# Last step of the block inverse split over both 64-partition halves, and the sample tokens' z with both parts of the rows in one left side

## The chip, the cores and the metric

The kernel runs on one core of one Trainium2 chip. The time is device time in microseconds (us) of one execution; a run is repeated and the median is given. The engines are named as in the profile: PE is TensorE's matmuls, PEld its weight loads (the left side of a matmul), DVE is VectorE, ACT is ScalarE, POOL is GpSimd, SP is SyncE, which here issues the DMAs.

## The reference

One inference step of one decoder layer, on a prompt of 2048 tokens and on 8 sample sequences of 4 tokens each (32 rows, which go along with the last pass over the prompt). An input projection of 1024 columns feeds two head groups: 16 state-space heads (SSD) and 8 gated delta-rule heads (GDN), each with a gate z that is a column block of the same projection.

```
h    = rmsnorm(x) * (1 + scale) + shift
proj = h @ w_in                       # z_s, xbc, dt, z_g, qkv, a, b
# GDN, in chunks of rows, per head:
M    = strict_lower((k*beta) @ k.T * decay);   A = I + M
u, w = solve(A, [v*beta, k*beta*exp(gcum)])    # unit lower triangular
v_new = u - w @ S;  o = q_dec @ S + attn @ v_new;  S = S*d + k_dec.T @ v_new
# SSD: y = chunked state-space scan, then y * silu(z_s), norm
o    = rmsnorm(o) * silu(z_g)
out  = x + gate * (concat(y, o) @ w_out);      y = rmsnorm(out)
```

The kernel uses chunks of 128 rows and forms the inverse of A for each chunk and head, by blocks: the four 32 x 32 diagonal blocks first, then pairs of them, then the 64 x 64 block off the diagonal. This last block is a product of three 64 x 64 matrices, made in two steps of one matrix product each.

## The kernel before

The prompt goes through in four passes of 512 tokens. All work of the passes is cut into small functions, each put at a due time with `at(tau, f)`; one unit of tau is a quantum, about one half of a projection tile, and a pass is 106 of them. The functions are run in order of tau. TensorE's instructions stay in just that order (`manual_schedule`); the other engines' order is made by the framework's scheduler from its own model of the times. SP issues nearly all DMAs, in one queue.

The projections are made with fp32r matmuls on parts: each fp32 value is a high part and a low part (`hhi`, `hlo` for the normed rows, two halves of a tile for the weights), and a product is high x high, high x low and low x high, added up in PSUM. `z_pair` makes two z tiles of 128 columns each in four quanta; in the last pass (`p == SP`) each quantum also makes the z of the 32 sample rows, into a PSUM buffer `d["s"]` that stays over the four quanta. `zmm` is the product of one slice k: three matmuls, with the rows as the left side (128 prompt rows, or 32 sample rows) and 256 weight columns moving. There are 8 z pairs, so 32 quanta in the last pass. At the end of a pair the z tiles go through ACT (tanh) and DVE (multiply-add); the sample's goes to `zsd` in DRAM.

`gdn_pair` carries two heads (b = 0, 1) through a pass: 4 chunks each, so 8 matrices in `U` (column index c = 4 b + chunk). After the diagonal blocks come the functions `b2_0` to `b2_4`: b2_0 transposes blocks, b2_1 and b2_2 make the 32 x 32 blocks off the diagonal in each 64 x 64 half, b2_3 and b2_4 the 64 x 64 block. b2_3 multiplies into partitions 64 to 127 of a PSUM buffer, ACT copies that to `p2x`; b2_4 multiplies into partitions 0 to 63 of another, DVE copies that into `U`. The functions b2_1 to b2_4 stand 1.45 quanta apart. After them come the `hop`s, three a chunk, which carry the state S through the chunks and read U in the second. There are 4 pairs in each of 4 passes, 16 in all.

PSUM has eight buffers: three of tag `ip` (projections), three of tag `bk` (b2, transposes, SSD chunks, the sample's z, and more, in turn), one `ch` and one `o` (hops). `ssd_group` has the SSD chunks; its function `second` (L1035) makes 8 heads' products of 64 columns, each in two matmuls of 64 left columns, one to partitions 0 to 63 and one to 64 to 127. `want` loads and splits the weights, four halves ahead (`NH = 4`). After the passes comes the output projection (L1185), with the sample tokens' own scans woven in.

Of the kernel before, what the change touches and what calls it, by code (L numbers as in the profile page):

```python
# [7 lines left out]
F32 = mybir.dt.float32  # L8
F32R = mybir.dt.float32r
AF = mybir.ActivationFunctionType  # L10
ALU = mybir.AluOpType
X = mybir.AxisListType.X

P = 128
DM = 1024
SEQ = 2048
KD = 8
T = 512
NPC = SEQ // T
NC = T // P  # L20
NS = 32
# [8 lines left out]
def _bc(ap, shape):  # L30
    while len(ap.shape) < len(shape):
        ap = ap.unsqueeze(len(ap.shape))
    return ap.to_broadcast(shape)
# [3 lines left out]
def hymba_step_kernel(  # L37
# [6 lines left out]
    v, s, g, pe = nc.vector, nc.scalar, nc.gpsimd, nc.tensor  # L44
    cnt = [0]

    def nm(t):
        cnt[0] += 1
        return f"{t}_{cnt[0]}"

    def mk(pool, shape, tag, dt=F32):
        return pool.tile(shape, dt, tag=tag, name=nm(tag))
# [13 lines left out]
    def psum(tag):  # L66
        return pools[tag].tile([P, 512], F32, tag=tag, name=nm("p" + tag))
# [20 lines left out]
    ct = const.tile([P, KD, 9], F32, name="ct")  # L88
# [28 lines left out]
    hw = ph1.enter_context(tc.tile_pool(name="hw", bufs=1))  # L117
    wp = ph1.enter_context(tc.tile_pool(name="wp", bufs=NH))
    xr = ph1.enter_context(tc.tile_pool(name="xr", bufs=3))
    keep = ph1.enter_context(tc.tile_pool(name="keep", bufs=1))  # L120
# [4 lines left out]
    trp = ph1.enter_context(tc.tile_pool(name="trp", bufs=4))  # L125
# [5 lines left out]
    def at(tau, f):  # L131
        events.append((tau, len(events), f))
# [16 lines left out]
            yield  # L149


    th9 = keep.tile([P, KD, 9], F32, name="th9")
    sc = keep.tile([P, KD, 9], F32, name="sc")
    s.activation(th9[:], ct[:], AF.Tanh, scale=0.5)
    v.tensor_scalar(sc[:], ct[:], 0.5, None, ALU.mult)
    v.scalar_tensor_tensor(sc[:], th9[:], 1.0, sc[:], ALU.add, ALU.mult)
    ADA = ("kT", "vs", "qd", "kd", "A", "U")
    ada_n = [0]

# [42 lines left out]
        return part  # L202


    hhi = hw.tile([P, KD, T + NS], F32R, name="hhi")
    hlo = hw.tile([P, KD, T + NS], F32R, name="hlo")
    wg2 = keep.tile([P, KD, 64], F32R, name="wg2")
    id2 = keep.tile([64, 32], F32, name="id2")
# [10 lines left out]
    dt2 = keep.tile([P, 8, 64], F32, name="dt2")  # L219
    p1x = keep.tile([P, 8, 64], F32, name="p1x")  # L220
    p2x = keep.tile([P, 8, 64], F32, name="p2x")
# [14 lines left out]
    def split(hi, lo, src):  # L236
        s.copy(hi, src)
        v.tensor_tensor(lo, src, hi, ALU.subtract)  # L238

    def rstd(ssq, n, scale):  # L240
        w = ssq.shape[1]
        m = mk(b2, [P, NC], "m1")[0:n, 0:w]
        v.tensor_scalar(m, ssq, scale, EPS, ALU.mult, ALU.add)
        r = mk(b2, [P, NC], "r1")[0:n, 0:w]
        rsq(r, m)
        return r
# [7 lines left out]
    def row_stats(src, n, ss, pool, tag):  # L254

        sh = mk(b2, [P, 2], "ssq2")
        xs = []
        for i in range(2):
            xt = mk(pool, [P, T], tag)
            nc.sync.dma_start(xt[0:n], src[:, i * 512:(i + 1) * 512])  # L260
            jk = mk(b1, [P, 512], "xsq", mybir.dt.bfloat16)
            s.activation(jk[0:n], xt[0:n], AF.Square, accum_out=sh[0:n, i:i + 1])
            xs.append(xt)
        v.tensor_tensor(ss, sh[0:n, 0:1], sh[0:n, 1:2], ALU.add)
        return xs
# [51 lines left out]
    def h_sample():  # L317
        ss = mk(b2, [P, 1], "ssq")[0:NS]
        xs = row_stats(x_s, NS, ss, xr, "xin")
        r = rstd(ss, NS, 1.0 / DM)  # L320
        pt = psum("bk")
        for i in range(2):
            v.tensor_scalar(xs[i][0:NS], xs[i][0:NS], r, None, ALU.mult)
            for k in range(4 * i, 4 * i + 4):
                pe.transpose(pt[:, k * NS:(k + 1) * NS], xs[i][0:NS, (k - 4 * i) * P:(k - 4 * i + 1) * P],
                             ident[0:NS, 0:NS])
        hv = mk(trp, [P, T], "tr")[:, 0:KD * NS]
        h4 = hv.rearrange("p (k b t) -> p k b t", k=KD, b=NB)
        v.tensor_tensor(h4, pt[:, 0:KD * NS].rearrange("p (k b t) -> p k b t", k=KD, b=NB),
                        _bc(s1[:, :, 1:9], [P, KD, NB, 4]), ALU.mult)  # L330
        v.tensor_tensor(h4, h4, _bc(mod[:, 0:8, 1:9], [P, KD, NB, 4]), ALU.add)
        split(hhi[:, :, T:T + NS], hlo[:, :, T:T + NS], hv.rearrange("p (k t) -> p k t", k=KD))

    state = {}

# [123 lines left out]
    n = 0  # L459
# [57 lines left out]
    def fill(tau, parts):  # L517
        d = {}
        fills.append((tau, parts, d))
        return d  # L520
# [63 lines left out]
    def z_pair(tau, n, p, mcol, done):  # L584

        d = fill(tau, [(n, j, True) for j in range(4)])

        def quantum(j):
            want(d["i0"] + j)
            ws = [w.rearrange("p (t k) c -> p t k c", t=2) for w in wt[d["i0"] + j]]  # L590
            for bk in range(2):
                if j == 0:
                    d[bk] = psum("ip")
                for k in range(2 * j, 2 * j + 2):
                    for i in range(2):
                        c = bk * 2 + i
                        cols = slice(c * P, (c + 1) * P)
                        zmm(d[bk][:, i * 256:(i + 1) * 256], k, cols, ws, i == 0)
            if p == SP:
                if j == 0:  # L600
                    d["s"] = psum("bk")
                for k in range(2 * j, 2 * j + 2):
                    zmm(d["s"][0:NS, 0:256], k, slice(T, T + NS), ws, True)
            if j == 3:
                zt = mk(b4, [P, NC, 256], "z")
                for bk in range(2):
                    zf = zt[:, bk * 2:bk * 2 + 2, :].rearrange("p a b -> p (a b)")
                    s.activation(zf, d[bk][:], AF.Tanh, scale=0.5)
                    v.scalar_tensor_tensor(zf, zf, 1.0, d[bk][:], ALU.add, ALU.mult)
                if p == SP:  # L610
                    zs_ = mk(trp, [P, T], "tr")[0:NS, 0:256]
                    s.activation(zs_, d["s"][0:NS, 0:256], AF.Tanh, scale=0.5)
                    v.scalar_tensor_tensor(zs_, zs_, 1.0, d["s"][0:NS, 0:256], ALU.add, ALU.mult)
                    nc.sync.dma_start(zsd[:, mcol:mcol + 256], zs_)
                done(zt)

        def zmm(out, k, cols, ws, first):
            for e, (a, b) in enumerate(((hhi, 0), (hhi, 1), (hlo, 0))):
                pe.matmul(out.rearrange("p (t c) -> p t c", t=2), a[:, k, cols], ws[b][:, :, k % 2, :],  # L619
                          start=(first and k == 0 and e == 0), stop=(k == KD - 1 and e == 2), skip_group_check=True)  # L620

        for j in range(4):
            at(tau + j, lambda j=j: quantum(j))


    def gdn_pair(p, pr, so, zq, e, dch):
# [225 lines left out]
        def b2_3():  # L852
            U = st["U"]
            pw = psum("bk")
            for c in range(8):
                pe.matmul(pw[64:128, c * 64:(c + 1) * 64], U[:, c, 64:128], dt2[:, c, :], start=True, stop=True)
            s.copy(p2x[64:128], pw[64:128, :].rearrange("p (c n) -> p c n", c=8))

        def b2_4():
            U = st["U"]  # L860
            pz = psum("bk")
            for c in range(8):
                pe.matmul(pz[0:64, c * 64:(c + 1) * 64], p2x[:, c, :], U[:, c, 64:128], start=True, stop=True)
            v.tensor_copy(U[0:64, :, 64:128], pz[0:64, :].rearrange("p (c n) -> p c n", c=8))

        at(so + 31.7 + e, b2_0)
        for i, f in enumerate((b2_1, b2_2, b2_3, b2_4)):
            at(so + 33 + e + 1.45 * i, f)
# [192 lines left out]
    for p in range(NPC):  # L1061
# [30 lines left out]
        if p + 1 < NPC:  # L1092
            for tt in range(NC):
                at(base + 60.4 + 4 * tt, lambda p=p, tt=tt: stat_tile(p + 1, tt, xr, "xin"))
            sr = stat_row(p + 1)
            for i in range(2):
                at(base + (93.6, 96.4)[i], lambda sr=sr: next(sr))
            if p + 1 == SP:
                at(base + 94.4, h_sample)
# [598 lines left out]
```

## Time and profile before

| | |
|---|---|
| median of 3 runs | 2328.43 us (2324.95 to 2330.56) |
| the profiled execution | 2327.78 us, span 2326.1 us |
| mean granted TensorE clock | 0.979 |
| TensorE matmuls | 15405, busy 2200.8 us (95% of the span) |
| weight loads | busy 1864.9 us (80%) |
| VectorE, ScalarE, GpSimd | 1481.9 (64%), 953.1 (41%), 826.7 us (36%) |
| DMA | 387.94 MB, mean 167 GB/s |

A busy TensorE is not one at its peak: a matmul's duration contains its way through the array, and the next begins before it ends, so what a group of matmuls takes from the program is read from the distance of their starts. In a group line of the profile stand line, engine, operation, tile written and tiles read, shapes (partitions x columns of the left side, then of the moving side), count, busy time, mean duration of one, and the idle time of the engine ahead of them with what ended it. An fp32 matmul of the program is two instructions in the profile, an fp32r one is one.

### The profile page before, as it was taken

How to read it: one execution, taken by the hardware profiler on the slowest of the kernel's cores; microseconds unless marked ns; L12 is line 12 of the kernel's file. 1: busy time of each engine (PE TensorE's matmuls, PEld its weight loads, DVE VectorE, ACT ScalarE, POOL GpSimd, SP SyncE). 2: the span in 40 equal slices, each digit the busy share in tenths (PEclk: the TensorE clock that was granted, in tenths of full speed). 3: DMA queues.
4: the chain of work that ended last, by engine and by line, in shares of the span. 5: the costliest groups of instructions: out<-in, count | busy, mean ns of one | idle time of the engine just before them, and what ended most of it. 6: DMA issues, size and time to landing. Idle time of an engine off the chain costs nothing. (4 is left out here: it accounts for less than half of the span.)

```text
span 2326.1 us, 41856 instructions
## 1 busy us (share of the span) xinstructions
PE 2200.8 (95%) x15405; PEld 1864.9 (80%) x15405; DVE 1481.9 (64%) x3574; ACT 953.1 (41%) x2680; POOL 826.7 (36%) x1052
## 2 busy tenths in 40 slices
PE   6999999989999999999999989999999799998998
PEld 3688878868897887889788889998899377786786
DVE  2466868786767768675666776668676564454323
ACT  2534556454536445442533453435433432231111
POOL 3255665554437243411522241215211554322000
PEclk8999999999999999999999999999999999999999
DMA  6354655555766675465645544555445563643321
GB/s 239 113 167 152 191 166 180 181 181 174 225 214 209 213 225 183 143 193 165 191 153 179 178 135 132 180 154 157 150 147 160 165 211 125 191 155 128 129 86 52
DMA packets 241112, 387.94 MB, mean 167 GB/s; under 512 B 75880, under 2 KB 132968, under 8 KB 240908
## 3 DMA queue, kind: packets, MB, share of 16 engines
q1 hardware_dynamic: 240908, 385.28, 52.2%
q8 instruction: 121, 1.98, 0.3%
q14 instruction: 83, 0.68, 0.1%
HBM read 289.89 MB, written 95.30 MB: 166 GB/s over the span
## 5 line engine op out<-in xcount | busy, mean ns | idle before, releaser
L531 PE MATMUL pip<-hhi,w 128*128 128x512 f32 (+1 forms) x2880 | 823.7, 362 | 6.7 <-DVE kT L549 4.9
L531 PEld LDWEIGHTS pip<-hhi,w 128*128 128x128 f32 x2880 | 515.0, 190 | 85.0 <-issue 6.9
L531 PE MATMUL pip<-hlo,w 128*128 128x512 f32 (+1 forms) x1440 | 509.8, 354 | 0.0
L619 PE MATMUL pip<-w,hhi 128*128 128x256 f32 x2048 | 382.6, 287 | 0.3 <-DVE cv L549 0.3
L496 POOL TENSOR_TENSOR w<-xin,w 128x512 fp32r<-128x512 f32 x156 | 202.6, 1301 | 378.3 <-ACT w L495 344.8
L619 PEld LDWEIGHTS pip<-w,hhi 128*128 128x128 f32 x2048 | 316.5, 190 | 2.4 <-DVE cv L549 0.5
L531 PEld LDWEIGHTS pip<-hlo,w 128*128 128x128 f32 x1440 | 274.5, 191 | 36.9 <-issue 4.5
L619 PE MATMUL pip<-w,hlo 128*128 128x256 f32 x1024 | 289.4, 283 | 0.0
L1185 PE MATMUL pip<-wohi,mh 128*128 128x512 f32 x480 | 195.3, 407 | 7.4 <-ACT mh L1169 7.2
L619 PEld LDWEIGHTS pip<-w,hlo 128*128 128x128 f32 x1024 | 194.8, 190 | 0.0
L1185 PE MATMUL pip<-wohi,ml 128*128 128x512 f32 x480 | 189.7, 395 | 1.1 <-DVE ml L1176 1.0
L1185 PE MATMUL pip<-wolo,mh 128*128 128x512 f32 x480 | 189.1, 394 | 0.8 <-DVE wolo L238 0.8
L539 DVE SCALAR_TENSOR_TENSOR tr<-pip,cw,tr 128x509 f32<-128x509 f32 (+5 forms) x240 | 152.8, 637 | 40.2 <-ACT tr L536 37.1
L539 DVE SCALAR_TENSOR_TENSOR cv<-pip,cw,cv 128x509 f32<-128x509 f32 (+2 forms) x180 | 114.7, 637 | 44.6 <-ACT cv L536 42.5
L1000 POOL TENSOR_TENSOR L<-L,g_gc 128x512 f32<-128x512 f32 x64 | 70.9, 1120 | 198.4 <-DMA L<-rowsd 198.1
L495 ACT CAST w<-xin 128x512 fp32r<-128x512 f32 x156 | 95.1, 612 | 80.9 <-PE pip L619 25.9
L795 DVE TENSOR_TENSOR tl<-dl,ul 128x60 f32<-128x60 f32 (+21 forms) x432 | 121.0, 280 | 9.3
L797 DVE TENSOR_TENSOR dl<-dl,tl 128x60 f32<-128x60 f32 (+21 forms) x432 | 119.1, 276 | 9.0
L1185 PEld LDWEIGHTS pip<-wohi,mh 128*128 128x128 f32 x480 | 91.4, 190 | 27.0 <-ACT mh L1169 7.8
L1185 PEld LDWEIGHTS pip<-wohi,ml 128*128 128x128 f32 x480 | 91.0, 190 | 22.8 <-DVE ml L1176 3.0
L1185 PEld LDWEIGHTS pip<-wolo,mh 128*128 128x128 f32 x480 | 91.4, 190 | 18.2 <-DVE wolo L238 1.1
L1169 ACT CAST mh<-pch 128x512 fp32r<-128x512 f32 (+1 forms) x60 | 33.7, 562 | 166.4 <-PE pch L1166 166.3
(433 smaller groups left out, 4141.3 us busy)
## 6 DMA issues: line engine op xcount, KB each, us to landing
w<-wsp SPq DMA_DIRECT2D x260, 512.0 KB
wsp<-w SPq DMA_DIRECT2D x104, 512.0 KB
xin<-in_w_in SPq DMA_DIRECT2D x156, 256.0 KB
L<-rowsd SPq DMA_DIRECT2D x64, 256.0 KB
mx<-mixd SPq DMA_DIRECT2D x28, 512.0 KB
E<-rowsd SPq DMA_DIRECT2D x32, 256.0 KB
ul<-ud SPq DMA_DIRECT2D x64, 128.0 KB
mixd<-z SPq DMA_DIRECT2D x16, 512.0 KB
```

The costliest lines, as they stand in the source:

```text
L495: mark("ACT", s.copy(hi, rv))
L496: mark("POOL", g.tensor_tensor(lo, rv, hi, ALU.subtract))
L531: pe.matmul(pp, a[:, k, :], b[:, kk, cols], start=(i == 0), stop=(i == 23))
L539: v.scalar_tensor_tensor(u[:, c0 + dd:c0 + w], pp[:, 0:w - dd], cw[:, ci, k:k + 1], u[:, c0 + dd:c0 + w], ALU.mult, ALU.add)
L619: pe.matmul(out.rearrange("p (t c) -> p t c", t=2), a[:, k, cols], ws[b][:, :, k % 2, :], start=(first and k == 0 and e == 0), stop=(k == ...
L795: v.tensor_tensor(tmp[:, 0:r, 0:w], _bc(dl[:, 0:r, m], [P, r, w]), ul[:, m, m + 1:32].unsqueeze(1).to_broadcast([P, r, w]), ALU.mult)
L797: v.tensor_tensor(dl[:, 0:r, m + 1:32], dl[:, 0:r, m + 1:32], tmp[:, 0:r, 0:w], ALU.add)
L1000: g.tensor_tensor(L[:], L[:], _bc(G()["gc"][:, gi * 8 + q * 4:gi * 8 + q * 4 + 4, c], [P, 4, P]), ALU.subtract)
L1169: s.copy(mh[:, :, 0:n], ptv)
L1185: pe.matmul(pos[hb][0:m, :], a[:, k, 0:m], b[q * 4 + k][:, hb * 512:(hb + 1) * 512], start=(q == 0 and k == 0 and j == 0), stop=(q == 3 an ...
```

## The change

Two parts of the kernel's matmuls are laid out anew.

In b2_3 and b2_4 the eight products go in the order of chunks, and for each chunk one of head 0 and one of head 1. The two heads' results lie in different halves of the PSUM partitions, in the same columns (256 in place of 512). Each result is then copied in two instructions, one a head; the one whose partitions differ from those of the target moves them in the copy.

For the sample rows' z, `hhi` gets 32 more columns, into which the low parts of the sample rows are copied once. The left side of the product with the high weights is then 64 columns, high and low rows side by side, and the product with the low weights has 32 as before: two matmuls a slice in place of three. The high x high (and high x low) sums come out in partitions 0 to 31, low x high in 32 to 63; at the end of a pair ACT copies the latter, DVE adds them, and the tanh and the multiply-add go on from the sum in SBUF. `th9`, a small early tile, moves from a pool of its own into the ring of the `tr` tiles to make room.

```diff
-    th9 = keep.tile([P, KD, 9], F32, name="th9")
+    th9 = mk(trp, [P, T], "tr")[:, 0:KD * 9].rearrange("p (k c) -> p k c", c=9)
...
-    hhi = hw.tile([P, KD, T + NS], F32R, name="hhi")
+    hhi = hw.tile([P, KD, T + 2 * NS], F32R, name="hhi")
...
         split(hhi[:, :, T:T + NS], hlo[:, :, T:T + NS], hv.rearrange("p (k t) -> p k t", k=KD))
+        v.tensor_copy(hhi[:, :, T + NS:T + 2 * NS], hlo[:, :, T:T + NS])
...
+                sv = d["s"][:, 0:256].rearrange("p (t c) -> p t c", t=2)
                 for k in range(2 * j, 2 * j + 2):
-                    zmm(d["s"][0:NS, 0:256], k, slice(T, T + NS), ws, True)
+                    for m, b in ((2 * NS, 0), (NS, 1)):
+                        pe.matmul(sv[0:m], hhi[:, k, T:T + m], ws[b][:, :, k % 2, :], start=(k == 0 and b == 0),
+                                  stop=(k == KD - 1), skip_group_check=True)
...
-                    zs_ = mk(trp, [P, T], "tr")[0:NS, 0:256]
-                    s.activation(zs_, d["s"][0:NS, 0:256], AF.Tanh, scale=0.5)
-                    v.scalar_tensor_tensor(zs_, zs_, 1.0, d["s"][0:NS, 0:256], ALU.add, ALU.mult)
+                    zs_ = mk(trp, [P, T], "tr")[0:NS, 0:512]
+                    zt_, zs_ = zs_[:, 256:512], zs_[:, 0:256]
+                    s.copy(zt_, d["s"][NS:2 * NS, 0:256])
+                    v.tensor_tensor(zt_, d["s"][0:NS, 0:256], zt_, ALU.add)
+                    s.activation(zs_, zt_, AF.Tanh, scale=0.5)
+                    v.scalar_tensor_tensor(zs_, zs_, 1.0, zt_, ALU.add, ALU.mult)
...
             pw = psum("bk")
-            for c in range(8):
-                pe.matmul(pw[64:128, c * 64:(c + 1) * 64], U[:, c, 64:128], dt2[:, c, :], start=True, stop=True)
-            s.copy(p2x[64:128], pw[64:128, :].rearrange("p (c n) -> p c n", c=8))
+            for c in range(4):
+                cc = slice(c * 64, (c + 1) * 64)
+                for e in range(2):
+                    o = 64 * (1 - e)
+                    pe.matmul(pw[o:o + 64, cc], U[:, e * 4 + c, 64:128], dt2[:, e * 4 + c, :], start=True, stop=True)
+            for e in range(2):
+                o = 64 * (1 - e)
+                s.copy(p2x[64:128, e * 4:e * 4 + 4, :], pw[o:o + 64, 0:256].rearrange("p (c n) -> p c n", c=4))
...
             pz = psum("bk")
-            for c in range(8):
-                pe.matmul(pz[0:64, c * 64:(c + 1) * 64], p2x[:, c, :], U[:, c, 64:128], start=True, stop=True)
-            v.tensor_copy(U[0:64, :, 64:128], pz[0:64, :].rearrange("p (c n) -> p c n", c=8))
+            for c in range(4):
+                cc = slice(c * 64, (c + 1) * 64)
+                for e in range(2):
+                    pe.matmul(pz[64 * e:64 * e + 64, cc], p2x[:, e * 4 + c, :], U[:, e * 4 + c, 64:128], start=True,
+                              stop=True)
+            for e in range(2):
+                v.tensor_copy(U[0:64, e * 4:e * 4 + 4, 64:128],
+                              pz[64 * e:64 * e + 64, 0:256].rearrange("p (c n) -> p c n", c=4))
```

More of the change, by code (lines that the diff above doesn't have):

```diff
@@ L149, in hold @@
             yield
-    th9 = keep.tile([P, KD, 9], F32, name="th9")
+    th9 = mk(trp, [P, T], "tr")[:, 0:KD * 9].rearrange("p (k c) -> p k c", c=9)
     sc = keep.tile([P, KD, 9], F32, name="sc")
-    s.activation(th9[:], ct[:], AF.Tanh, scale=0.5)
+    s.activation(th9, ct[:], AF.Tanh, scale=0.5)
     v.tensor_scalar(sc[:], ct[:], 0.5, None, ALU.mult)
-    v.scalar_tensor_tensor(sc[:], th9[:], 1.0, sc[:], ALU.add, ALU.mult)
+    v.scalar_tensor_tensor(sc[:], th9, 1.0, sc[:], ALU.add, ALU.mult)
     ADA = ("kT", "vs", "qd", "kd", "A", "U")
```

## The prediction

> **What bounds the kernel now.** I read the page's engine shares first, then busy time by stage (windows of one pass each), then TensorE's waits. The first two rows are busy time of each engine and, in 40 slices, TensorE's busy tenths; the rows from 120.00 on are stages (length, then busy time and instructions per engine, granted clock, DMA share, GB/s), the four passes over the tokens and their sum.
>
> ```profile
> PE 2200.8 (95%) x15405; PEld 1864.9 (80%) x15405; DVE 1481.9 (64%) x3574; ACT 953.1 (41%) x2680; POOL 826.7 (36%) x1052
> PE   6999999989999999999999989999999799998998
> ...
> 120.00:520.00 400.00, 378.76 (x2685) 323.84 (x2683) 296.12 (x666) 201.91 (x522) 228.64 (x249) 0.97 0.55 176
> 520.00:940.00 420.00, 409.34 (x3003) 351.43 (x3002) 308.76 (x729) 205.00 (x573) 183.49 (x222) 1.00 0.65 205
> 940.00:1360.00 420.00, 405.03 (x2999) 353.62 (x2998) 290.74 (x746) 181.81 (x530) 119.09 (x170) 0.98 0.55 170
> 1360.00:1800.00 440.00, 426.08 (x3893) 407.53 (x3892) 301.58 (x927) 178.53 (x608) 105.63 (x145) 1.00 0.49 152
> sum 1680.00, PE 1619.20 PEld 1436.41 DVE 1197.21 ACT 767.25 POOL 636.85; mean PE 404.80 PEld 359.10 DVE 299.30 ACT 191.81 POOL 159.21
> ...
> PE pbk L1035 <- ACT p1x L837: 8.5, 3, 4.8
> PE pip L1185 <- ACT mh L1169: 7.2, 1, 7.2
> PE pbk L856 <- DVE L L1025: 4.0, 2, 3.0
> ```
>
> In the 1680 us of the passes TensorE is idle for 1680.00 - 1619.20 = 60.8 us, spread over more than forty waits; no other engine is above three quarters busy and DMA stays at 0.65 or less. The waits that exist (the last three rows: total, times, longest) are single late buffers. TensorE's program, written out in order, is the bound, so time taken out of it should come off the end unless it is taken out just ahead of a wait on something not paced by TensorE.
>
> **The last step of the block inverse (b2_3, b2_4): a gain of 15.3 us.** The groups by shape and three bursts in the timeline (start, us, engine, line):
>
> ```profile
> L1035 PE MATMUL pbk<-xdt,L 128*64 128x64 f32 x1024 | 38.4, 231 | 8.5 <-ACT p1x L837 8.5
> L863 PE MATMUL pbk<-U,p2x 128*64 128x64 f32 x256 | 18.3, 225 | 0.0
> L856 PE MATMUL pbk<-dt,U 128*64 128x64 f32 x256 | 18.2, 225 | 4.0 <-DVE L L1025 4.0
> ...
> L856 PE MATMUL pbk<-dt,U x256: 222/222/270, 208.9 to 1802.3; 128*64 128x64 f32 x128
> ...
> 307.97 1.15 PE L856 MATMUL pbk<-dt,U 128*64 128x64 f32 x16
> 309.04 0.50 PE L531 MATMUL pip<-hhi,w 128*128 128x512 f32 x1
> 311.17 0.58 ACT L857 COPY p2x<-pbk 64x512 f32<-64x512 f32 x1
> 312.02 1.15 PE L863 MATMUL pbk<-U,p2x 128*64 128x64 f32 x16
> ...
> 1817.39 1.15 PE L1035 MATMUL pbk<-xdt,L 128*64 128x64 f32 x32
> ```
>
> L856 and L863 run once in each of 16 pair passes, 8 calls in 16 instructions (each fp32 call is two), all into the same 64 output partitions. One matmul is 0.222 long, so 16 in 1.15 start (1.15 - 0.222) / 15 = 0.062 apart. L1035 has the same shape (128 rows, 64 weight columns, 64 moving columns, fp32), but its calls alternate between output partitions 0 to 63 and 64 to 127: 32 in the same 1.15, or 0.928 / 31 = 0.030 apart. The change gives the two lines just that alternation, head against head. A burst's last start then comes after 15 x 0.030 = 0.449 instead of 0.928, 0.48 us sooner. With 32 bursts (2 lines x 16) that is 15.3 us. The ends of this term are zero (no overlap, see the rivals) and 15.3; I take 15.3, since the row of L1035 is the same form.
>
> **z of the sample tokens: a gain of 7.5 us.** A quantum in the last pass (TensorE alone; L619 into pbk is the sample part, 32 weight columns):
>
> ```profile
> L619 PE MATMUL pbk<-w,hhi x128: 276/276/281, 1403.8 to 1791.2; 128*32 128x256 f32 x128
> L619 PE MATMUL pbk<-w,hlo x64: 276/276/285, 1404.0 to 1791.3; 128*32 128x256 f32 x64
> ...
> 1403.65 0.28 PE L619 MATMUL pip<-w,hlo 128*128 128x256 f32 x1
> 1403.77 0.40 PE L619 MATMUL pbk<-w,hhi 128*32 128x256 f32 x2
> 1404.01 0.28 PE L619 MATMUL pbk<-w,hlo 128*32 128x256 f32 x1
> 1404.12 0.39 PE L619 MATMUL pbk<-w,hhi 128*32 128x256 f32 x2
> 1404.35 0.28 PE L619 MATMUL pbk<-w,hlo 128*32 128x256 f32 x1
> 1404.47 0.60 PE L896 MATMUL pch<-vp,kd 128*128 128x128 f32 x4
> ```
>
> 128 + 64 = 192 instructions, six a quantum in 32 quanta. Six take from 1403.77 to 1404.47, 0.117 each. The change issues four: both parts of the rows against the high weights in one 64-column left side, the high rows against the low weights in one of 32. Two fewer a quantum, 2 x 32 x 0.117 = 7.5 us. Left sides of 128 columns (the L619 row at 1403.65, next start 0.12 later) stream 256 columns at the same pace as those of 32, so I price one of 64 no higher.
>
> What the trace of before does not have is a change between left sides of 64 and 32 columns. Its nearest row is the step from 128 to 32 at 1403.65 to 1403.77, and from 32 back to 128 at 1404.35 to 1404.47: 0.12 each, no more than between equals. The other end is the step out of the L856 burst: the last of 16 starts at 307.97 + 0.928 = 308.90, and L531 only at 309.04, 0.14 later against 0.062 inside it, so 0.08 extra. A quantum has two changes of width now (128 to 32, 32 to 128) and five after (128, 64, 32, 64, 32, 128). Three more in 32 quanta at 0.08 are 7.7 us, which would eat this term whole: the range of z is +0.2 to -7.5. I take -7.5, by the nearer row (same type, same step of the program).
>
> **What the copies cost.** Each evacuation becomes two halves of 64 x 256:
>
> ```profile
> L857 ACT COPY p2x<-pbk x16: 581/583/585, 210.1 to 1802.5; 64x512 f32<-64x512 f32 x16
> L864 DVE COPY U<-pbk x16: 672/683/684, 216.4 to 1812.7; 64x512 f32<-64x512 f32 x16
> 1798.32 0.36 ACT L850 COPY U<-pbk 32x256 f32<-32x256 f32 x1
> 1797.25 0.42 DVE L848 COPY dt<-pbk 32x256 f32<-32x256 f32 x1
> L612 ACT ACTIVATE tr<-pbk x8: 357/374/375, 1424.1 to 1791.6; 32x256 f32<-32x256 f32 x8
> L613 DVE SCALAR_TENSOR_TENSOR tr<-tr,pbk x8: 398/402/402, 1425.5 to 1792.2; 32x256 f32<-32x256 f32 x8
> L238 DVE TENSOR_TENSOR hlo<-tr,hhi x1: 426/426/426, 1279.8 to 1279.8; 128x256 fp32r<-128x256 f32 x1
> ```
>
> ACT: 2 x 0.36 - 0.58 = 0.14 more, DVE: 2 x 0.42 - 0.68 = 0.16 more, 16 times each: 2.2 and 2.6 us, on engines with 900 and 480 us to spare in the passes. What counts is who stands behind them. L863 needs both halves of p2x. At 311.17 the copy started late and ended at 311.75, 0.27 ahead of L863; with the first burst 0.48 sooner and two copies, the second half would end near 311.9 and L863 would reach for it near 311.6: a stall of 0.3 to 0.4. By the same two rows the other pairs have 0.8 to 5 us. I book 0.5 us. If that cover were gone everywhere it would be 16 x 0.4 = 6.4. The second half of U is needed by the second hop, a hop's distance away; nothing is booked, and the buffer pz stays taken 0.16 longer.
>
> For z, a copy on ACT (0.36) and an add on DVE (about 0.40) come before the tanh. The PSUM buffer is let go after copy and add, where before it was after tanh and multiply-add (0.37 + 0.40), so no longer. The store to zsd leaves some 0.8 later, 8 times, and SyncE's queue behind it with the weight loads: 6.4 us if none were covered; they run four halves ahead, and a pass of 106 quanta takes about 420 us, 4 us each, so nothing is booked. The added copy of the low rows (0.43, by the L238 row) is one DVE instruction; its columns are first read by z at 1403.77, some 120 us on. The wider hhi costs room only, th9 in the ring of tr is read at once; both nothing.
>
> **What of the gain is lost.** In TensorE's timeline only one of the bursts is followed within 8 us by a wait of TensorE over 0.2 us, the last:
>
> ```profile
> 1805.19 1.15 PE L863 MATMUL pbk<-U,p2x 128*64 128x64 f32 x16
> 1809.63 1.10 PE L1044 MATMUL pbk<-xdt,sct 128*128 128x512 f32 x2 [3.29 <-DVE L L1025]
> ...
> 1810.73 2.06 DVE L238 TENSOR_TENSOR wolo<-x,wohi 128x1024 fp32r<-128x1024 f32 x1
> 1812.72 0.67 DVE L864 COPY U<-pbk 64x512 f32<-64x512 f32 x1
> ```
>
> There, in the tail of the last pass, VectorE sets the pace (U is copied 6.4 us after its burst), so this pair's two savings, 1.0 us, are gone. For the rest, faster bursts that run into waits elsewhere and other engines' work being lined up anew, I book 1.9 us; its bounds are 0 and a third of the 60.8, 20 us, of which I take the small end because of that row.
>
> Sum: -15.3 - 7.5 + 0.5 + 1.0 + 1.9 = **-19.4 us**. The profiled execution took 2327.78 (span 2326.1); the median of three runs is 2328.43, 0.65 more. 2327.78 - 19.4 = 2308.4 for an execution like it, and against the median **2309**. A change of 0.2%, 4.7 us, is about what measurement can tell from none.
>
> **The rivals.**
> Changes of width make TensorE wait (A). If each change had to wait for the matmul ahead to leave, it would cost 0.276 - 0.117 = 0.16; three more in 32 quanta are 15.3 us, z turns from -7.5 to +7.8, and the sum is -4.1: 2324. Against it stand the two steps of 0.12 above. The Trainium skill, TensorEngine Tiling (Array Packing), section Tiling Modes, Key Properties, says that a change of tiling mode drains TensorE; by that rule A holds. The trace does not agree for the steps between 128 and 32 columns, and has no step from 64 to 32.
>
> No overlap in the bursts (B), so that the change doesn't do what it says. The pairs of L1035 read the same moving columns in both halves; those of b2_3 and b2_4 read different ones. Then 15.3 is zero and z alone stays, with nothing lost in bursts: 2328.4 - 7.5 + 1.0 = 2322. Against it:
>
> ```profile
> 288.13 0.70 PE L834 MATMUL pbk<-dtx,U 128*32 128x32 f32 x32
> L834 PE MATMUL pbk<-dtx,U x512: 190/196/217, 189.4 to 1793.7; 128*32 128x32 f32 x171
> ```
>
> L834 alternates two output groups with different moving columns, 32 wide, (0.70 - 0.196) / 31 = 0.016 apart: a quarter of 0.062 at half the width, as overlap needs.
>
> The second half-copy holds the bank (C, the other sign). The three bk buffers are turned over by ACT and DVE; the wait at L1035 on p1x (8.5 us in 3, 4.8 the longest) shows what a late copy costs. If the scheduler puts other work between the halves, TensorE waits at the next psum("bk"). It takes (22.8 + 4.7) / 32 = 0.86 us per burst to come out slower; a 2.06 us piece ran ahead of the U copy at 1812.72. Every burst hit so and by one us is +9: 2338. Against it: no wait follows 31 of the bursts, and the halves can go at once.
>
> The gain is met by new waits (D): a third of the 60.8 grows back, -22.8 + 1.5 + 15 = -6: 2322.
>
> **How the numbers follow.** Forecast with its costs within the bounds, 0.80; A 0.05; B 0.04; D 0.06; C 0.05. Low end: the whole 22.8, and 3.5 more where an earlier bk buffer shortens waits like L1035's 8.5, 2302. High end: z at nothing (+7.5) on 2309 is 2316.5; reaching on over half of B and D, 2321. Faster by over 0.2% (under 2323.7) holds the forecast, B, D, 0.90, less 0.01 for their tails: 0.89. Same: A and half of C's weak form, 0.07. Slower: 0.04.
>
> **What will show it.** The x16 bursts of b2_3 and b2_4 at about 0.67 (15 x 0.030 + 0.222) instead of 1.15: right; near 1.15: B. L619's sample part at four instructions a quantum in 0.47, 64 fewer in all (15341 TensorE matmuls): right; 0.70 and more: A. TensorE idle in the passes near 63 us: right; 75 or more: D. Waits at bk lines named after the half-copies: C. I would be wrong, too, if the tail from 1800 on, where TensorE waits for others, stretches.

## The result, and the profile after

The changed kernel took 2310.7 us (2305.23 to 2314.97, four runs) beside 2328.9 us of the kernel before on the same chip: a ratio of 0.9923, 95% interval 0.9897 to 0.9949. Twice more, each time beside the kernel before, the ratios were 0.993 (0.9913 to 0.9946) and 0.9918 (0.9904 to 0.9931). In microseconds of the medians: 18.2, 17.0 and 19.8 less. The forecast was 19.4 less, 2309.0. A ratio is an estimate of its own with an interval, not the quotient of the two medians, so the two can differ by a few microseconds. Three single executions of the variants below took 2704, 5248 and 6410 us and are left out of the medians.

The page of the changed kernel's profiled execution (2312.91 us, span 2311.2), engine shares and TensorE's busy tenths:

```profile
PE 2183.9 (94%) x15341; PEld 1849.9 (80%) x15341; DVE 1491.0 (65%) x3599; ACT 958.0 (41%) x2704; POOL 821.1 (36%) x1052
PE   7998999989999998999999989999999799999998
```

There are 64 matmuls fewer, as many as the sample's z was to lose. Its groups by shape (L866 and L877 are b2_3 and b2_4, L606 is the sample's z, L869 and L880 are the copies to `p2x` and `U`):

```profile
L877 PE MATMUL pbk<-U,p2x 128*64 128x64 f32 x256 | 11.3, 228 | 0.8 <-ACT p2x L869 0.8
L866 PE MATMUL pbk<-dt,U 128*64 128x64 f32 x256 | 10.9, 227 | 4.0 <-DVE L L1042 4.0
...
L606 PE MATMUL pbk<-w,hhi 128*32 128x256 f32 x64 | 16.5, 280 | 0.0
L606 PE MATMUL pbk<-w,hhi 128*64 128x256 f32 x64 | 16.5, 280 | 0.0
...
L880 DVE COPY U<-pbk 64x256 f32<-64x256 f32 x32 | 13.4, 418 | 2.7 <-PE pbk L877 2.4
L869 ACT COPY p2x<-pbk 64x256 f32<-64x256 f32 x32 | 11.7, 366 | 10.8 <-PE pbk L866 10.2
```

One instruction of a burst is as long as before (0.227 us, before 0.225); the busy time of a line fell from 18.2 to 10.9 because the instructions now lie over one another. The timeline (start, us, engine, line) gives the distance to the next work, first for a burst, then for z:

```profile
310.69 0.69 PE L866 MATMUL pbk<-dt,U 128*64 128x64 f32 x16
311.31 0.19 PEld L532 LDWEIGHTS pip<-hhi,w 128*128 128x128 f32 x1
311.31 0.50 PE L532 MATMUL pip<-hhi,w 128*128 128x512 f32 x1
...
1398.45 0.29 PE L626 MATMUL pip<-w,hlo 128*128 128x256 f32 x1
1398.57 0.63 PE L606 MATMUL pbk<-w,hhi 128*64 128x256 f32 x4
1399.04 0.61 PE L913 MATMUL pch<-vp,kd 128*128 128x128 f32 x4
```

A burst holds the program for 0.62 us, where it was 309.04 - 307.97 = 1.07: 0.46 less (0.61 to 0.62 against 1.07 to 1.08 in nearly all of them), 32 times, 14.7 us. Four z matmuls take 0.47. Six took 0.70 in the quantum that the prediction shows, but this is the first of 32 and the longest. The next one is the rule; TensorE in the kernel before:

```profile
1408.21 0.39 PE L619 MATMUL pbk<-w,hhi 128*32 128x256 f32 x2
1408.44 0.28 PE L619 MATMUL pbk<-w,hlo 128*32 128x256 f32 x1
1408.55 0.39 PE L619 MATMUL pbk<-w,hhi 128*32 128x256 f32 x2
1408.78 0.28 PE L619 MATMUL pbk<-w,hlo 128*32 128x256 f32 x1
1408.89 0.49 PE L877 MATMUL pch<-sg,kT 128*128 128x128 f32 x3
```

These six take 0.68. Added up over the 32 quanta, the sample's z held the program for 21.9 us before and holds it for 15.1 now: 6.8 us less. With the bursts that is 21.5 us taken out of TensorE's program. How much of it arrived is seen in stages (length, busy time of each engine, clock): from the first work of the first pass to the last burst of b2_3, from there to the output projection, and the rest. Before:

```profile
104.10:1801.30 1697.20, 1636.40 (x12703) 1451.49 (x12703) 1208.77 (x3086) 779.95 (x2276) 648.15 (x798) 0.99 0.56 175
1801.30:1859.40 58.10, 41.03 (x285) 22.10 (x279) 34.79 (x66) 24.66 (x71) 35.68 (x46) 0.93 0.53 172
1859.40:2326.10 466.70, 442.47 (x2140) 346.86 (x2140) 205.11 (x353) 111.25 (x265) 114.74 (x161) 0.98 0.42 134
```

The same three stages of the changed kernel:

```profile
105.90:1788.50 1682.60, 1617.69 (x12641) 1433.71 (x12641) 1216.34 (x3108) 783.16 (x2294) 646.91 (x796) 0.98 0.57 177
1788.50:1847.10 58.60, 41.86 (x283) 22.73 (x277) 35.74 (x69) 26.32 (x77) 31.23 (x47) 0.89 0.51 164
1847.10:2311.20 464.10, 441.04 (x2140) 346.65 (x2140) 205.92 (x353) 111.36 (x264) 115.28 (x161) 0.99 0.42 135
```

The passes are shorter by 14.6 us in this execution, and TensorE's idle time in them is 1682.60 - 1617.69 = 64.9 us, where it was 60.8. These two profiled executions alone (14.9 apart in the span) would say that almost a third of the 21.5 was lost. The section on the clock below shows where it went.

### The profile page after: what moved, and what is told of

Same layout as the page of the kernel before. It is cut to its first block, busy times and chain, and to the rows that moved or that the text cites. A ratio compares the mean times of both kernels' runs of the same rounds, so it can differ in the third digit from the quotient of the medians.

```text
span 2311.2 us, 41793 instructions
## 1 busy us (share of the span) xinstructions
PE 2183.9 (94%) x15341; PEld 1849.9 (80%) x15341; DVE 1491.0 (65%) x3599; ACT 958.0 (41%) x2704; POOL 821.1 (36%) x1052
## 5 line engine op out<-in xcount | busy, mean ns | idle before, releaser
L532 PE MATMUL pip<-hhi,w 128*128 128x512 f32 (+1 forms) x2880 | 823.3, 363 | 6.0 <-DVE kT L550 4.8
L532 PEld LDWEIGHTS pip<-hhi,w 128*128 128x128 f32 x2880 | 516.0, 191 | 83.1 <-issue 6.5
L532 PE MATMUL pip<-hlo,w 128*128 128x512 f32 (+1 forms) x1440 | 509.4, 354 | 0.0
L532 PEld LDWEIGHTS pip<-hlo,w 128*128 128x128 f32 x1440 | 275.2, 191 | 35.5 <-issue 4.5
L804 DVE TENSOR_TENSOR dl<-dl,tl 128x60 f32<-128x60 f32 (+21 forms) x432 | 124.0, 287 | 9.0
L496 ACT CAST w<-xin 128x512 fp32r<-128x512 f32 x156 | 95.0, 613 | 77.7 <-POOL w L497 21.5
L1202 PEld LDWEIGHTS pip<-wolo,mh 128*128 128x128 f32 x480 | 91.4, 190 | 18.2 <-DVE wolo L238 1.1
```

Source lines behind the costliest of these rows:

```text
L496: mark("ACT", s.copy(hi, rv))
L532: pe.matmul(pp, a[:, k, :], b[:, kk, cols], start=(i == 0), stop=(i == 23))
L804: v.tensor_tensor(dl[:, 0:r, m + 1:32], dl[:, 0:r, m + 1:32], tmp[:, 0:r, 0:w], ALU.add)
L1202: pe.matmul(pos[hb][0:m, :], a[:, k, 0:m], b[q * 4 + k][:, hb * 512:(hb + 1) * 512], start=(q == 0 and k == 0 and j == 0), stop=(q == 3 an ...
```

## The experiments

**Each half alone.** First the burst change by itself (the diff's b2_3 and b2_4, nothing else of it):

```diff
-            for c in range(8):
-                pe.matmul(pw[64:128, c * 64:(c + 1) * 64], U[:, c, 64:128], dt2[:, c, :], start=True, stop=True)
...
+            for c in range(4):
+                cc = slice(c * 64, (c + 1) * 64)
+                for e in range(2):
+                    o = 64 * (1 - e)
+                    pe.matmul(pw[o:o + 64, cc], U[:, e * 4 + c, 64:128], dt2[:, e * 4 + c, :], start=True, stop=True)
```

> The change to b2_3 and b2_4 alone; z of the sample tokens as before. Theory (the bursts alternate between output halves and overlap, 32 of them 0.46 us shorter by the changed kernel's profile, 1.08 to 0.62 to the next start): 14.7 us of TensorE's program gone, some 2 us of it lost in waits, so about 2316, ratio 0.9945. The x16 bursts at 0.69, the sample's z at six matmuls a quantum in 0.70. Rival (the gain comes mostly from z, and the half-copies eat what the bursts give): 2325 or more, ratio 0.998 or more.

Measured: 2318.94 beside 2332.91, ratio 0.9934 (0.9921 to 0.9948), 14.0 us less, with bursts that hold the program for 0.61 to 0.62 us. Then z by itself: the four-matmul form, its extra columns and the copy, with b2_3 and b2_4 as before (`for c in range(8)`).

> The sample tokens' z with both parts in one left side, and the room for it; b2_3 and b2_4 as before. Theory: 64 matmuls fewer at 0.117 are 7.5 us, the changes of width cost nothing, so about 2322, ratio 0.997; a quantum's sample part 0.47 to the next start. Rival (changes between left sides of 64 and 32 columns cost 0.08 to 0.16 each): 2329 to 2337, the sample part at 0.70 or more.

Measured: 2326.38 beside 2332.91, 6.5 us less by the medians; the ratio, 0.9959 (0.9944 to 0.9975), says 9.6. The product of the two ratios is 0.9893, and the whole change had given 0.9923 and 0.993; so either some 6 us are lost only where both stand together, or the ratios scatter by that much. All three were put beside one another on one chip:

> The burst change alone, again. 14.7 us less in the bursts, about 1.4 of stalls and 1 in the tail: 0.9947 by the matmuls. The first time it was 0.9934; if that holds, the gain alone is larger than its matmuls and part of it is the clock's.

> The z change alone, again. 7.4 us less: 0.9968. The first time it was 0.9959, 9.5 us.

> The changed kernel once more, beside its two halves on one chip, to see whether the two gains add. If they add, this ratio is the product of the other two less what the faults of additivity cost within the scatter: by the matmuls taken out, 14.7 us (bursts) and 7.4 us (z), less about 2 of stalls, 0.9913. If about 6 us are lost only where both changes stand together (new waits and half-clock stretches), 0.993 again, and the product of the two halves is below it by 0.002 or more.

Measured: 0.9957 (0.9945 to 0.997; 10.9 us), 0.9961 (0.9946 to 0.9975; 7.7 us), both 0.9918 (0.9904 to 0.9931; 19.8 us). The product of the first two is 0.9918: the two gains add, and nothing is lost by their standing together that this measurement can tell. In the two sets the bursts gave 14.0 and 10.9 of their 14.7 us by the medians, and z 6.5 and 7.7 of its 6.8 (the expectations say 7.4, from the first quantum). In between the changed kernel alone was run once more:

> The changed kernel once more, beside the kernel before, to see whether the two parts add up. Alone the inverse took 0.66% (0.9934) and z 0.41% (0.9959). Theory (TensorE's program is the bound, so they add, less a part lost in waits): ratio 0.990 to 0.991, 21 to 23 us. Rival (what one frees the other can't use, the first comparison's 0.9923 was the true value): 0.992 to 0.993, 16 to 18 us.

Measured: 2316.56 beside 2333.55, 0.993, as told above. That is the rival's value; the 0.990 to 0.991 of the theory lie just below its interval. Beside its halves the whole came out at 0.9918, with the bursts alone at 0.9957 where the first time they had been at 0.9934: the first measurement of the halves had promised too much.

**What in the burst makes the gain: the order of the heads.** The two output halves stay and only the order of the products is turned back, all of head 0 and then all of head 1:

```diff
-            for c in range(4):
-                cc = slice(c * 64, (c + 1) * 64)
-                for e in range(2):
-                    o = 64 * (1 - e)
+            for e in range(2):
+                o = 64 * (1 - e)
+                for c in range(4):
+                    cc = slice(c * 64, (c + 1) * 64)
```

> The changed kernel, but in b2_3 and b2_4 all four products of one head come first and then the four of the other: the same instructions, halves, and copies, without the alternation. Theory (alternation makes neighbours overlap): the bursts are back at about 1.15, at most one pair of neighbours overlaps, and of the whole gain only z's stays, less 2 x 0.15 per pair for copies where they show: about 2322 to 2324, ratio 0.997 to 0.998. Rival (smaller output range or two halves as such make the gain): as fast as the changed kernel, 2311, bursts near 0.69.

The timeline of this kernel, burst and next matmul:

```profile
306.31 0.97 PE L866 MATMUL pbk<-dt,U 128*64 128x64 f32 x16
307.20 0.50 PE L532 MATMUL pip<-hhi,w 128*128 128x512 f32 x1
```

Time 2321.69, 0.9943 (0.9929 to 0.9958). The burst holds the program for 0.89 us, not for 1.07 as forecast, nor for 0.62: a miss. The recorded starts of its 16 instructions tell how it comes: the distances (ns) are 106, 59, 58, 58, 6, 53, 54, 4, 54, 4, 54, 59, 58, 58, 59. In the middle, where one half's products end and the other's begin, three starts come only 4 to 6 ns after another; the rest stand 53 to 59 apart. Before, all but the first step (107) are 58 or 59. The trace doesn't tell which half an instruction writes, but the reading that fits is that the first instructions of the second half begin among the last of the first: the one behind the first step of 6 ns takes 270 ns, like the first of the burst, and the others 222. In the changed kernel the distances are 6 or 7 and 51 or 52 by turns in most bursts: two instructions, one in each half, go as a pair. So what counts is a neighbour in the other half, and some three instructions around the seam find one even without the alternation. If they can, pairs of products must do nearly as well as single ones:

```diff
-            for c in range(4):
-                cc = slice(c * 64, (c + 1) * 64)
-                for e in range(2):
+            for c2 in (0, 2):
+                for e, c in ((0, c2), (0, c2 + 1), (1, c2), (1, c2 + 1)):
+                    cc = slice(c * 64, (c + 1) * 64)
```

> The changed kernel with the products in the order of two of one head, two of the other, and so on. The run with the heads in turn showed three starts of the second head among the last of the first, 0.17 us saved a burst. Theory (TensorE looks some three instructions ahead to the other half): runs of four instructions nearly all find a partner, a burst comes to 0.62 to 0.70 to the next start and the time is that of the changed kernel. Rival (only direct neighbours overlap): three boundaries of one pair each, 1.08 - 3 x 0.052 = 0.92.

The timeline of this kernel:

```profile
308.48 0.73 PE L866 MATMUL pbk<-dt,U 128*64 128x64 f32 x16
309.14 0.50 PE L532 MATMUL pip<-hhi,w 128*128 128x512 f32 x1
```

0.66 us to the next matmul (0.66 or 0.67 in most), and a time of 2314.01 (two executions), 0.9916 (0.9894 to 0.9938): of the 0.46 that the alternation saves, 0.41 to 0.42 come with two and two.

**The changes of width in z (rival A).** Both sample matmuls get the 64-column left side, so that three changes of width in a quantum go:

```diff
-                    for m, b in ((2 * NS, 0), (NS, 1)):
+                    for m, b in ((2 * NS, 0), (2 * NS, 1)):
```

The sum then holds the low rows times the low weights too, which the other kernels leave out.

> The changed kernel with 64 columns in the left side of both sample products of z (the low rows against the low weights are added too), so that there is no change from 64 to 32 columns inside a quantum; the count of matmuls is the same. Theory (changes of width cost nothing): four matmuls in 0.47 as in the changed kernel, the same time. Rival (each change costs up to 0.08): 0.23 less in each of 32 quanta, 7 us faster.

The timeline, with z between its neighbours:

```profile
1393.07 0.28 PE L626 MATMUL pip<-w,hlo 128*128 128x256 f32 x1
1393.18 0.63 PE L606 MATMUL pbk<-w,hhi 128*64 128x256 f32 x4
1393.65 0.61 PE L913 MATMUL pch<-vp,kd 128*128 128x128 f32 x4
```

0.47 from the first of the four to the next work; the mean of the 32 quanta is 0.464, against 0.472 with widths that change, which makes 0.3 us in all and not the 7 of the rival. The time is 2313.1 (two executions), 0.9912 (0.9889 to 0.9935). The mean steps between the matmuls are 113 to 114 ns with 32 columns throughout (before), 114 to 116 with 64 throughout and 118 to 119 where the width changes. The Trainium skill, TensorEngine Tiling (Array Packing), section Tiling Modes, Key Properties, says that a change of tiling mode drains TensorE; in this kernel neither the steps from 128 to 32 columns nor those from 64 to 32 show it (0.11 to 0.12 us each, where waiting for the matmul ahead would be 0.28). That each such step is a change of mode in the page's sense isn't shown.

**The half-copies (rival C).** Each pair of copies is spread over both engines, ACT and DVE:

```diff
-                s.copy(p2x[64:128, e * 4:e * 4 + 4, :], pw[o:o + 64, 0:256].rearrange("p (c n) -> p c n", c=4))
+                (v.tensor_copy if e else s.copy)(p2x[64:128, e * 4:e * 4 + 4, :],
+                                                 pw[o:o + 64, 0:256].rearrange("p (c n) -> p c n", c=4))
...
-                v.tensor_copy(U[0:64, e * 4:e * 4 + 4, 64:128],
-                              pz[64 * e:64 * e + 64, 0:256].rearrange("p (c n) -> p c n", c=4))
+                (s.copy if e else v.tensor_copy)(U[0:64, e * 4:e * 4 + 4, 64:128],
+                                                 pz[64 * e:64 * e + 64, 0:256].rearrange("p (c n) -> p c n", c=4))
```

> The changed kernel with the half-copies shared out: of p2x one half by ScalarE and one by VectorE, of U likewise, so that the halves can go at the same time. Theory (the copies are covered but for one or two bursts, 0.5 us booked, 0.8 us of waits on p2x seen): no change from the changed kernel within 2 us, ratio to before 0.990 to 0.993. Rival (the second half-copy holds bk buffers and costs some of the 4 us that went missing): 3 to 5 us faster than the changed kernel.

TensorE's waits in this kernel (total, times, longest):

```profile
PE pbk L878 <- DVE p2x L869: 3.2, 3, 1.9
PE pbk L878 <- ACT p2x L869: 1.2, 2, 0.8
```

and in the changed kernel:

```profile
PE pbk L1052 <- ACT p1x L844: 7.3, 3, 3.4
...
PE pbk L877 <- ACT p2x L869: 0.8, 1, 0.8
PE pbk L1032 <- ACT p2x L869: 0.6, 1, 0.6
```

Two engines for the two halves make b2_4 wait longer (4.4 us for 0.8), most of it for the half on VectorE (3.2). The time is 2313.99, 0.991 (0.9886 to 0.9934), beside 2316.56 for the changed kernel on the same chip: 2.6 less, between what theory and rival asked for and not to be told from nothing, so the times don't decide and the waits must. The wait of 0.8, in the changed kernel:

```profile
1584.24 0.75 ACT L869 COPY p2x<-pbk 64x256 f32<-64x256 f32 x2
1584.66 1.07 PE L877 MATMUL pbk<-U,p2x 128*64 128x64 f32 x16 [0.79 <-ACT p2x L869]
1585.65 0.40 PE L532 MATMUL pip<-hhi,w 128*128 128x272 f32 x1
```

TensorE waits for the first half, whose copy started late; then the burst stops after two instructions until the second half is there, and holds the program for 1.00 in place of 0.62. So the second copy costs 0.38 us here. The second execution of the changed kernel, of which more below, has two such places:

```profile
PE pbk L877 <- ACT p2x L869: 1.5, 2, 0.8
```

In the changed kernel's first execution one wait of 0.6 us is of the kind that rival C speaks of, a buffer that the second half-copy still holds (at 1794.4, in the tail). There is no other in this trace.

**The room for z.** The kernel before with the wider `hhi`, the copy into it and `th9` in the ring of `tr`, and no other part of the change:

```diff
-    th9 = keep.tile([P, KD, 9], F32, name="th9")
+    th9 = mk(trp, [P, T], "tr")[:, 0:KD * 9].rearrange("p (k c) -> p k c", c=9)
...
+        v.tensor_copy(hhi[:, :, T + NS:T + 2 * NS], hlo[:, :, T:T + NS])
```

> The kernel before with only the room for the change: th9 in the ring of tr, 32 more columns in hhi and the copy of the low sample rows into them; all matmuls as before. Theory (costs nothing but one VectorE instruction of 0.29 us): no change, 2329, ratio 1.000 within 0.2%. Rival (the new layout and the order that the scheduler makes of it move waits about): off by 4 us or more to either side, with TensorE's instruction times as before and its idle time in the passes changed by as much from 60.8 us.

2335.76 beside 2332.91, 1.0007 (0.9994 to 1.0019): nothing that can be told from none, as the prediction booked it. But its passes, as a window, show what the rival names:

```profile
104.10:1805.50 1701.40, 1636.72 (x12712) 1453.39 (x12712) 1214.39 (x3089) 781.20 (x2284) 647.65 (x798) 0.99 0.57 175
```

TensorE idles 1701.40 - 1636.72 = 64.7 us in them, as long as in the changed kernel (64.9) and 3.9 longer than before (60.8), with no faster burst in the program. The burst change alone, which has none of the room, has 65.4 and 62.6 in two executions. Two executions of one program differ by 2.8 here and there is one trace of the kernel before, so a growth of 4 us can't be put down to a part of the change.

## Where the third of the gain in the first profile went: mostly the clock

The changed kernel was profiled again beside its halves, and this execution has a span of 2302.3 us, 8.9 less than the first one of the same program. Its cores' view:

```profile
core 0: 2302.3 us, clock 0.980
```

the first line of its page:

```profile
PE 2174.8 (94%) x15341; PEld 1844.0 (80%) x15341; DVE 1488.2 (65%) x3599; ACT 959.7 (42%) x2704; POOL 823.1 (36%) x1052
```

its passes, as a window:

```profile
103.50:1779.60 1676.10, 1612.11 (x12643) 1430.73 (x12643) 1212.78 (x3107) 784.69 (x2294) 649.30 (x796) 0.99 0.57 177
```

and the cores' view of the first execution:

```profile
core 0: 2311.2 us, clock 0.976
```

TensorE idles as long in both (2311.2 - 2183.9 = 127.3, 2302.3 - 2174.8 = 127.5); it is the same 15341 matmuls that took 9.1 us longer. The granted clock accounts for that: (1 - 0.976) x 2311.2 = 55.5 us were not granted in the one, (1 - 0.980) x 2302.3 = 46.0 in the other, 9.4 apart (the clock is given to three places, so each by 1.2 either way).

The trace's record of the granted clock has two values only, 1 and 0.50. The stretches at 0.50 are whole multiples of 3.41 us long (only the last is cut off by the end), and within each of the three traces (before and these two) their starts lie at whole multiples of 3.413 us from the first, to within 0.05 us. In the passes there are 13 such periods before, 15 in the first execution after and 12 in this one; each costs up to half its length, 1.7 us. With TensorE's idle time that gives the account of the passes:

| us | before | after, first | after, again |
|---|---|---|---|
| length of the passes | 1697.2 | 1682.6 | 1676.1 |
| difference | | -14.6 | -21.1 |
| matmuls taken out (30 bursts, z) | | -20.6 | -20.6 |
| TensorE idle | 60.8 | 64.9 (+4.1) | 64.0 (+3.2) |
| half-clock periods x 1.7 | 22.2 | 25.6 (+3.4) | 20.5 (-1.7) |
| left over | | -1.5 | -2.0 |

One place shows how the same wait makes a period in one execution and none in the other. Windows of 4 us (PEclk is the third number from the end), the first execution:

```profile
296.00:300.00 4.00, 1.99 (x11) 1.36 (x10) 1.21 (x3) 2.31 (x6) 3.52 (x4) 1.00 0.65 180
300.00:304.00 4.00, 3.53 (x57) 2.75 (x56) 3.96 (x9) 2.04 (x11) 2.51 (x2) 0.63 0.48 185
```

TensorE in the same two executions behind the same matmul of L532; the first:

```profile
299.63 0.63 PE L693 MATMUL pbk<-cs,tr 128*128 128x128 f32 x4 [2.01 <-DVE st L961]
...
301.55 0.80 PE L532 MATMUL pip<-hhi,w 128*128 128x512 f32 x1
302.15 0.63 PE L532 MATMUL pip<-hlo,w 128*128 128x512 f32 x1
302.57 1.05 PE L532 MATMUL pip<-hhi,w 128*128 128x512 f32 x2
```

and the second:

```profile
295.63 0.63 PE L693 MATMUL pbk<-cs,tr 128*128 128x128 f32 x4 [1.94 <-DVE st L961]
...
297.37 0.50 PE L532 MATMUL pip<-hhi,w 128*128 128x512 f32 x1
297.70 0.39 PE L532 MATMUL pip<-hlo,w 128*128 128x512 f32 x1
297.93 0.63 PE L532 MATMUL pip<-hhi,w 128*128 128x512 f32 x2
```

Waits of 2.01 and 1.94 us, and then matmuls of L532 at 0.42 us from one another in the one, at 0.23 in the other. In the first, the period of 3.41 us that ends at 301.0, where the clock falls, holds that whole wait and one of 0.47 behind it, 2.5 us idle. In the second the grid has a mark at 295.4, so the 1.94 us are cut, 1.7 ahead of it and 0.2 (with the 0.47, 0.7) behind, and the clock stays at 1. The Trainium skill, TensorE: Matmul & The Clock Gate, section Part 1: The HAM clock gate (the "warmup" mystery), tells of a free-running window of 3413 ns and of a clock that goes to a half after an idle window and to full after a busy one; the trace agrees in the length, in the two values and in the grid, and shows that such a period need not be idle throughout. In the three traces, from the first pass to the end, every period of the grid at full clock in which TensorE (by its matmul records) idled for more than 1.9 us of the 3.41 was followed by one at half clock (43 of 43), and none in which it idled for less than 1.5 (0 of 1219); in between it went either way (6 of 28).

So in the passes the first execution lost to idle time (4.1) and to two more periods of half clock (3.4). Over the whole span the clock is the larger part: (1 - 0.979) x 2326.1 = 48.8 us were not granted before, 55.5 in the first execution after, 6.6 more; TensorE's idle time there grew by 2.0 only (2326.1 - 2200.8 = 125.3, then 127.3). Together that is 8.6 us, 2.0 more than the 6.6 that are missing (21.5 - 14.9).

Run by run the same holds loosely: over the runs of the changed kernel the time goes with the time not granted (in the three sets of four, five and five runs with correlations of 0.91, 0.84 and 0.93), over those of the kernel before more weakly (0.36, 0.54 and 0.65). One execution of the one-width variant does not fit at all: its mean granted clock was 0.929, which would be some 113 us more not granted than in its other one (0.978), but it took 2315.07 us for 2311.13. It has no trace, and why is open. That the clock makes up all of the scatter isn't shown.

## Why the prediction was right, point by point

- **The bound.** Right: other engines' idle time and DMA changed nothing that could be found, and time taken out of TensorE's program came off the end but for a few microseconds.
- **The bursts, -15.3.** The mechanism holds. The burst takes 0.69 by the profile (0.67 was forecast) and frees the program 0.46 us sooner, for 0.48: 14.7 us. Even distances of 0.030 were inferred; in truth they are 6 and 52 ns by turns, with the same mean. Rival B (no overlap without a common moving tile) is refuted by the 0.62, and the heads in turn show that the alternation makes most of it: without it 0.18 us a burst stays, at the seam.
- **z, -7.5.** Right in kind, 0.7 too large: 6.8 in the trace, 6.5 and 7.7 by the medians of z alone. The price of 0.117 was read from the first quantum, the longest of the 32; the mean is 0.114 before and 0.118 after, where the widths change. Rival A is refuted in its size: 0.472 with the three changes of width, 0.464 without.
- **The copies.** Half a copy takes 0.37 on ACT and 0.42 on DVE, as the 32-partition rows had said. The stall of b2_4 on the second half of `p2x`, booked at 0.5, is 0.38 in the first execution, at 1584.66 and not at the pair that was pointed to. In the second there are two such bursts, at 1577.44 and, as the prediction said, at that pair (309.58), each holding the program for 1.00 in place of 0.62: 0.8 us. Not foreseen was that TensorE would also wait for the first half: 0.8 us in the first execution and 1.5 in the second, with 0.6 at L1032 in the tail of the first.
- **The last pair, +1.0.** In accord: the stage from its first burst to the output projection was 58.1, and is 58.6 and 59.4 in the two executions, though the bursts in it are 0.9 shorter. In the first execution TensorE waits behind the last burst for 3.3 us on POOL (`st`, L964), where before it was 3.3 on DVE. But the granted clock in the stage was lower too (0.93 before, 0.89 and 0.91), so how much of the saving the other engines took can't be told.
- **Waits elsewhere, +1.9.** Not shown. Idle time in the passes grew by 4.1 and 3.2 us, of which 0.5 had been booked for `p2x`, but the room alone has 3.9 more without a faster burst, so that this growth can't be put down to bursts running into waits. It lies below the 75 us that would have spoken for rival D.
- **What the sum left out.** The step that compared one profiled execution with another took the clock as given. Its periods moved the passes by +3.4 in one execution and by -1.7 in the other, more than any small term of the sum. The three differences of medians (18.2, 17.0, 19.8), which average over it, lie within 2.4 us of the forecast, which is closer than their own intervals resolve (3 to 6 us either way), so they don't test the small terms one by one; the two profiled executions, 14.9 and 23.8 us below the span of before, do not.

## What to carry to other kernels

Small fp32 products that leave half of the output partitions empty cost little more than half as much of TensorE's program (0.62 us a burst for 1.07 here) if two independent ones are placed in the two halves and issued by turns; the price is a second copy, 0.14 to 0.16 us of ACT or DVE, and 0.38 of TensorE where the copy comes late, here in one or two of 16 pairs. Price a repeated piece from all its repetitions and not from the first. Before explaining a difference of a few microseconds between two profiled executions, compare (1 - granted clock) x span and the half-clock periods in their traces: one period of half clock is 1.7 us here, and whether a wait of 2 us brings one depends on where it falls on their grid. When two parts of a change seem not to add, measure them beside each other on one chip before looking for the cause.

## What the runs showed of the hardware that was not expected

- Two 64-column fp32 products in different output halves start 6 or 7 ns apart, and the next pair 51 or 52 ns later in most bursts; in one half alone they start 58 to 59 apart. At a seam between halves, by the distances, three starts of the second half come in among the first half's last ones.
- The granted clock falls in periods of 3.41 us on a fixed grid, after each period at full clock in which TensorE idled for more than 1.9 us of the 3.41 and after none with less than 1.5. A few more or fewer of them, 1.7 us each, are as large as the small terms of this change.
